# Filler products of x by ones on TensorE in the first adaLN of a decoder layer: with and without

## The chip, the cores and the metric

The kernel runs on one core of a Trainium2 chip. The metric is device time in microseconds (us) of one execution. It stands beside the span that the hardware profiler shows, which runs from the program's first instruction to its last. TensorE is called PE in the profile, VectorE DVE, ScalarE ACT, GpSimd POOL and SyncE, which issues most transfers here, SP.

## What is computed

One layer of a decoder trunk, for a prompt of 512 tokens and 8 single-token samples that share the weights, so 520 columns of activations with 1024 rows. All is fp32 in and out. Cut to what matters here:

```
m  = silu(c) @ ada_w + ada_b                     # 1024 x 6144; one c for the prompt, 8 for the samples
shift1, scale1, gate1, shift2, scale2, gate2 = split(m, 6)
h  = RMSNorm(x) * (1 + scale1) + shift1
z  = h @ w_in                                    # q, k, v, recurrent branch, gates
A  = RG-LRU branch(z) @ w_proj_a
B  = forgetting attention(z, paged cache) @ w_proj_b
x  = x + gate1 * ((sigmoid(gA) * A + sigmoid(gB) * B) @ w_o)
x  = x + gate2 * SwiGLU(RMSNorm(x) * (1 + scale2) + shift2)
y  = RMSNorm(x)
```

The change stands in the first line and the second: in how shift1 and scale1 are made, ahead of the first h.

## The kernel before, in words

Activations lie transposed: 8 tiles of 128 rows by 520 columns, taken in two halves of 260 columns (HALF) for each product. A large product is made of three fp32r products (high part by high part, low weights by high activations, high weights by low activations); ACT makes the high parts of the weights, DVE the low parts. PSUM is a pool of 8 banks, one product of 260 columns in each, taken in turn. The instructions' order on each engine follows the program's text, with a few places set by hand through `issue_after`.

The program opens as follows. SP issues, in this order: the parameters and constants, the 8 tiles of x (L100), 8 loads `araw` of 512 KB each of the first adaLN's weights (L479, `first_mod(0, ...)`, one for each block kq of 128 rows of c), three loads `wraw` of the first q weights (L525), and the 8 `araw` of the second half (`first_mod(1, ...)`). The tiles `araw` share 7 buffers with the cache pages.

Meanwhile PE sums the squares of x over the partitions by a product with ones (L559, `ss`), and then makes shift1 and scale1 for the first four row blocks: `first_mod(0, ...)` makes, for each kq, four products `adaf` of a 32-column silu(c) by 256 columns of `araw`, side by side in the four column groups of the array (L482; an fp32 product stands as two instructions in the profile, so a block kq is "x8"). `first_mod_end(0, ...)` copies the sum (ACT, `adas`, L495), transposes it (PE, `adaft`, L498), adds the bias (DVE, `mod`, L504) and makes the amplitude (DVE, `n1amp`, L508). `first_h` then makes h tile by tile: its high part `hh` on ACT (L514 for the prompt's columns, L518 for the samples', which come by way of POOL, L515 and L516) and its low part `hl` on DVE (L517, L519). `q_weights` splits the q weights (`whi` on ACT, L532; `wlo` on DVE, L533). Then come the first products of q over four row blocks (`qp`, L542), in groups of six banks; the 8 blocks of the second half of adaLN (`adaf` again) stand between them.

Inside this stretch stands `keep_busy` (L488 to L491). It makes n further fp32 products on PE, `idle`, of a 128x128 matrix of ones by the first 260 columns of x, each behind the one before, into a bank of its own that nothing reads. `first_mod(0, ...)` calls it with n = 1 behind each block kq from 2 to 7 (L485 and L486), and `first_mod_end(0, ...)` with n = 3 behind the transposes (L499 and L500).

Of the kernel before, what the change touches and what calls it, by code (L numbers as in the profile page):

```python
# [28 lines left out]
HALF = NT // 2  # L29
# [36 lines left out]
def kernel(ctx, tc, xT, par, gates, b_f, cst, cse, own, cache_k, cache_v, cache_lf, pt,  # L66
# [3 lines left out]
    pe, act, dve, pool, sp = nc.tensor, nc.scalar, nc.vector, nc.gpsimd, nc.sync  # L70
# [9 lines left out]
    def slot(name, cols=NT, dt=F32, parts=128):  # L80
        return heap.tile([parts, cols], dt, name=name, tag="slot")

    def bank(name, parts=128, cols=512):
        return psp.tile([parts, cols], F32, name=name, tag="bank")
# [9 lines left out]
    x = []  # L94
# [9 lines left out]
    ident = cs[:, C_ID:C_ID + 128]  # L104
    ones = cs[:, C_ONE:C_ONE + 128]
# [5 lines left out]
    silc = keep.tile([128, KT, 32], F32, name="silc")  # L111
# [47 lines left out]
    for jt in range(FF // 128):  # L159
# [5 lines left out]
        for name in BLOCKS:  # L165
            units.append((c, name, 4))
            if name in JOIN[jt]:
                g, i = JOIN[jt][name]
# [307 lines left out]
    def first_mod(fh, acc, kqs):  # L476
        for kq in kqs:
            raw = pgp.tile([128, 2, 512], F32, name="araw", tag="pg")
            sp.dma_start(raw, ada_w[kq * 128:kq * 128 + 128, :2048].rearrange("p (v c) -> p v c", v=2)  # L479
                         [:, :, 512 * fh:512 * fh + 512])  # L480
            for g in range(4):
                m = pe.matmul(acc[32 * g:32 * g + 32, :256], lhsT=silc[:, kq],  # L482
                              rhs=raw[:, g // 2, 256 * (g % 2):256 * (g % 2) + 256],
                              start=kq == 0, stop=kq == KT - 1, tile_position=(0, 32 * g))
            if fh == 0:  # L485
                keep_busy(m, 1 if kq > 1 else 0)  # L486

    def keep_busy(m, n):  # L488
        for _ in range(n):
            with tc.issue_after(m.ins):  # L490
                m = pe.matmul(idle[:, :HALF], lhsT=ones, rhs=x[0][:, :HALF], start=True, stop=True)  # L491

    def first_mod_end(fh, acc):
        sb = slot("adas", 256)
        act.copy(sb, acc[:, :256])  # L495
        tp = bank(f"adaft{fh}")
        for b in range(2):
            m = pe.transpose(tp[:, b * 128:b * 128 + 128], sb[:, b * 128:b * 128 + 128], ident)  # L498
        if fh == 0:  # L499
            keep_busy(m, 3)  # L500
        tv = tp[:, :256].rearrange("p (b g c) -> p b g c", b=2, g=4)
        fs = slice(4 * fh, 4 * fh + 4)
        for v in (1, 0):
            dve.tensor_tensor(  # L504
                mod[:, v, fs].rearrange("p (q b) c -> p b q c", b=2), tv[:, :, 2 * v:2 * v + 2, 0:9],
                prm[:, fs, P_AB + v:P_AB + v + 1].rearrange("p (q b) c -> p b q c", b=2).to_broadcast([128, 2, 2, 9]),
                ALU.add)
        dve.scalar_tensor_tensor(amp1[:, fs], mod[:, 1, fs], 1.0, prm[:, fs, P_N1:P_N1 + 1].to_broadcast([128, 4, 9]),  # L508
                                 ALU.add, ALU.mult)
# [35 lines left out]
    def wraw():  # L545
        return wp.tile([128, KT, 256], F32, name="wraw", tag="wraw", bufs=2)

    idle = bank("idle")
    ssq = [bank(f"ss1_{j}") for j in range(2)]
    for f in range(KT):  # L550
        t = slot("sq1")
# [5 lines left out]
        if f % 4 == 3:  # L557
            for j, (t0, t1) in enumerate(HALVES):
                pe.matmul(ssq[j][:, :HALF], lhsT=ones, rhs=sq[:, t0:t1], start=f == 3, stop=f == KT - 1)  # L559
    acc = [bank(f"adaf{fh}") for fh in range(2)]  # L560
    first_mod(0, acc[0], range(KT))
    r1 = slot("r1")
    for j, (t0, t1) in enumerate(HALVES):
# [6 lines left out]
    raw = wraw()  # L570
    q_weights(0, raw, 0, 0)
    first_mod_end(0, acc[0])
    for f in range(4):
        first_h(f)
# [3 lines left out]
    for g3 in (0, 3):  # L578
        banks = [bank(f"qp{i}_{j}") for i in range(g3, g3 + 3) for j in range(2)]
        for k in range(4):  # L580
            for n in range(6):
                q_matmuls(0, g3 + n // 2, n % 2, k, banks[n])
                if g3 == 0 and n == 5:
                    first_mod(1, acc[1], (2 * k, 2 * k + 1))
            if g3 and k == 0:
                first_mod_end(1, acc[1])
                for f in range(4, KT):
                    first_h(f)
        for n in range(6):
            t0, t1 = HALVES[n % 2]  # L590
            act.copy(qpart[g3 + n // 2][:, t0:t1], banks[n][:, :HALF])
        if g3 == 0:
            flr = slot("flr", KT * H).rearrange("p (k c) -> p k c", k=KT)
            sp.dma_start(flr, w_in[:, COL_FL:COL_FL + H].rearrange("(k p) c -> p k c", p=128))
# [325 lines left out]
    for i in range(KT):  # L920
        if i % 4 == 0:
            qtp.append(bank(f"qt{i}", NS))
        if i < 6:
            t = qpart[i]
            for j, (t0, t1) in enumerate(HALVES):
                b = bank(f"q{i}_{j}")
# [52 lines left out]
    g = [None] * KT  # L979
# [397 lines left out]
    g = None  # L1377
# [323 lines left out]
    for j in range(2):  # L1701
        for m in range(2 * PLAIN):
            if j == 0:
                begin(u + 3)
            b = bank(f"fi{m}_{j}")
# [88 lines left out]
```

## Time and profile before

| | us |
|---|---|
| three runs | 1015.08, 1015.64, 1018.36 |
| median | 1015.64 |
| the profiled execution, its own time | 1018.03 |
| its span | 1016.4 |
| PE busy in the span | 994.3 |
| DVE busy | 797.3 |
| ACT busy | 547.5 |
| mean granted clock of TensorE | 0.996 |

Rows of the timeline have the start in us, the duration, the engine, the source line, the operation, the tile written and those read, the shape and the number of instructions merged; behind it in brackets the engine's idle time before it and what ended it. Rows of the chain of work have the start, the length and the work; the chain leads back from the last instruction to whatever released each one. "SPq" is SP's queue issuing a transfer; "to landing" is the time from there until the data are in place. A row of windows has a stretch's ends and its length, PE's busy time with its instructions, the granted clock of TensorE as a share of the full one, the busy share of the DMA engines and GB/s.

### The profile page before, as it was taken

What the parts mean: (1) busy time and instruction counts of PE and PEld (TensorE: products, weight loads), DVE (VectorE), ACT (ScalarE), POOL (GpSimd) and SP (SyncE); (2) the same over time, 40 slices, a digit from 0 to 9 for tenths busy, and PEclk for the clock granted to TensorE, in tenths of its full rate; (3) what the DMA queues carried; (4) which work ended last, traced back from release to release, by engine and by line L of the source; (5) the groups of instructions that cost most, each with busy time, mean ns of one, the idle gap of its engine ahead of it and who ended that gap; (6) DMA issues with size and microseconds to landing.
All of it is one profiled execution on the core that took longest, in us unless ns stands there. A gap on an engine that the chain in (4) does not pass through costs nothing.

```text
span 1016.4 us, 21281 instructions
## 1 busy us (share of the span) xinstructions
PE 994.3 (98%) x8012; PEld 921.1 (91%) x8012; DVE 797.3 (78%) x1423; ACT 547.5 (54%) x1128; POOL 327.6 (32%) x415
## 2 busy tenths in 40 slices
PE   5999999999999999999999999999999999999996
PEld 2799999999998988888888888999999999999996
DVE  5559999998999888886655544869988888888764
ACT  4534576848761576777783233554444444445553
POOL 0346111121143245653400001583442442425112
PEclk9999999999999999999999999999999999999998
DMA  9798857788879998995867995324234243233122
GB/s 325 250 324 279 242 189 202 243 261 278 281 250 345 331 312 286 321 294 190 251 216 269 319 340 186 84 74 115 81 108 125 63 125 98 70 104 105 63 64 85
DMA packets 164378, 206.97 MB, mean 204 GB/s; under 512 B 9827, under 2 KB 125043, under 8 KB 164211
## 3 DMA queue, kind: packets, MB, share of 16 engines
q1 hardware_dynamic: 147634, 152.78, 48.1%
q0 software_dynamic: 12960, 46.41, 13.8%
q10 hardware_dynamic: 3680, 6.42, 1.7%
q8 instruction: 63, 1.03, 0.4%
q14 instruction: 41, 0.33, 0.1%
HBM read 192.49 MB, written 13.09 MB: 202 GB/s over the span
## 4 chain that ended last, share of the span: by engine, by line
PE 93%; DMA 2%; DVE 2%; ACT 1%; issue 0%; SPq 0%; POOL 0%; DVEq 0%; POOLq 0%; ACTq 0%
PE fo L307 12%; PE k L307 5%; PE wo L307 5%; PE gb L307 5%; PE gr L307 5%; PE v L307 5%; PE ga L307 5%; PE xr L307 5%; PE pb L307 4%; PE pv L839 3%; PE pa L307 3%; PE po L1302 2%; PE qp L542 2%; PE q L542 2%; PE ada L374 2%; PE ptt L1268 2%
## 5 line engine op out<-in xcount | busy, mean ns | idle before, releaser
L246 ACT CAST whi<-wraw 128x1024 fp32r<-128x1024 f32 (+1 forms) x79 | 82.0, 1039 | 113.6 <-PE pb L307 34.3
L248 DVE TENSOR_TENSOR wlo<-wraw,whi 128x1024 fp32r<-128x1024 f32 (+1 forms) x79 | 99.1, 1256 | 19.0 <-ACT whi L246 16.6
L307 PE MATMUL fo<-ach,wb 128*128 128x260 f32 x512 | 93.4, 283 | 0.0
L270 ACT CAST wb<-ws 128x512 fp32r<-128x512 f32 x72 | 44.7, 621 | 86.0 <-PE fo L307 58.9
L700 POOL DMA_DIRECT2D pg<-in_cache_k_dram x74 | 39.6, 536 | 143.1 <-DVE S L751 62.6
L271 DVE TENSOR_TENSOR wb<-wraw,wb 128x512 fp32r<-128x512 f32 x86 | 76.4, 889 | 4.7 <-ACT wb L270 3.9
L307 PEld LDWEIGHTS fo<-ach,wb 128*128 128x128 f32 x512 | 78.9, 188 | 0.0
L271 DVE TENSOR_TENSOR wb<-ws,wb 128x512 fp32r<-128x512 f32 x72 | 68.7, 954 | 12.6 <-ACT wb L270 11.0
L261 POOL TENSOR_TENSOR ws<-wraw 128x512 f32<-128x512 f32 x18 | 24.4, 1353 | 153.2 <-DMA wraw<-in_w_fi_dram 104.1
L307 PE MATMUL fo<-acl,wb 128*128 128x260 f32 x256 | 72.2, 282 | 0.0
L270 ACT CAST wb<-wraw 128x512 fp32r<-128x512 f32 x86 | 53.5, 622 | 31.4 <-ACT cp L1683 6.2
L750 DVE TENSOR_TENSOR pg<-pg,qb 128x1024 f32<-128x1024 f32 x48 | 57.9, 1221 | 2.5 <-DMA pg<-in_cache_k_dram 2.5
L751 DVE TENSOR_REDUCE S<-pg 128x16 f32<-128x1024 f32 x48 | 57.4, 1209 | 0.2
L1259 POOL TENSOR_SCALAR p<-p,mu 128x128 f32<-128x128 f32 (+3 forms) x28 | 38.4, 1381 | 53.0 <-DVE mu L1255 47.1
L307 PEld LDWEIGHTS fo<-acl,wb 128*128 128x128 f32 x256 | 48.2, 188 | 0.0
L1253 ACT ACTIVATE p<-p,mu 128x128 f32<-128x128 f32 (+3 forms) x64 | 35.4, 554 | 18.2 <-DVE mu L1252 18.0
L307 PE MATMUL v<-hh,whi 128*128 128x260 f32 x128 | 38.2, 298 | 0.8 <-ACT row L819 0.5
L307 PE MATMUL k<-hh,whi 128*128 128x260 f32 x128 | 37.3, 292 | 0.0
L307 PE MATMUL pb<-oh,whi 128*128 128x260 f32 x128 | 37.1, 290 | 0.2 <-ACT oh L1360 0.2
L307 PE MATMUL gb<-hh,whi 128*128 128x260 f32 x128 | 37.0, 289 | 0.0
L307 PE MATMUL v<-hl,whi 128*128 128x260 f32 x128 | 36.9, 288 | 0.0
L307 PE MATMUL v<-hh,wlo 128*128 128x260 f32 x128 | 36.9, 288 | 0.0
(1101 smaller groups left out, 3957.3 us busy)
## 6 DMA issues: line engine op xcount, KB each, us to landing
araw<-in_ada_w_dram SPq DMA_DIRECT2D x48, 512.0 KB, 7.6
wraw<-in_w_fi_dram SPq DMA_DIRECT2D x44, 512.0 KB, 5.3
pg<-in_cache_k_dram POOLq DMA_DIRECT2D x42, 512.0 KB, 6.2
pg<-in_cache_v_dram SPq DMA_DIRECT2D x42, 512.0 KB, 5.5
wraw<-in_w_in_dram SPq DMA_DIRECT2D x34, 512.0 KB, 6.4
wraw<-in_w_in_dram SPq DMA_DIRECT2D x11, 1024.0 KB, 8.5
pg<-in_cache_v_dram POOLq DMA_DIRECT2D x22, 512.0 KB, 6.1
pg<-in_cache_k_dram POOLq DMA_DIRECT2D x32, 256.0 KB, 5.9
```

The lines of the kernel that those rows point to most:

```text
L246: state["act"] = act.copy(hi[:, :k1 - k0], src)
L248: state["last"] = dve.tensor_tensor(lo[:, :k1 - k0], src, hi[:, :k1 - k0].bitcast(F32), ALU.subtract)
L270: state["act"] = act.copy(t[:, :4], src)
L271: state["last"] = dve.tensor_tensor(t[:, 4:], src, t[:, :4].bitcast(F32), ALU.subtract)
L307: state["mm"] = pe.matmul(out[:, :t1 - t0], lhsT=wt[k], rhs=at, start=k == 0 and m == 0, stop=k == nk - 1 and m == 2)
L542: state["mm"] = pe.matmul(b[:, :HALF], lhsT=wt, rhs=at[:, t0:t1], start=k == 0 and m == 0, stop=k == 3 and m == 2)
L700: done.append(eng.dma_start(pg, cache[bass.ds(r, 1), :, c0:c1].rearrange("a p c -> (a p) c")))
L750: dve.tensor_tensor(pg, pg, q, ALU.mult)
L751: last = dve.tensor_reduce(S[r // 2][:, c:c + H], pg.rearrange("p (h d) -> p h d", d=DH), AX.X, ALU.add)
L839: pe.matmul(pv[0][32 * gq:32 * gq + 32, :], lhsT=pw[r][:, c:c + 32], rhs=pgs[gq // 2][:, 512 * hf:512 * hf + 512], start=j == 0, stop=j == ...
L1253: act.activation(p[:, :n + 128], p[:, :n + 128], AF.Exp, bias=mu[:, 0:1], scale=-1.0, accum_out=mu[:, 1:2])
L1259: (pool.tensor_scalar(p, p, mu[:, 2:3], None, ALU.mult) if a and i + 1 < KT else act.activation(p, p, AF.Copy, scale=mu[:, 2:3]))
```

## The change

The nine filler products, the function that makes them and their bank go. The other instructions keep their order on every engine; line numbers behind the function fall by 10 (L559 becomes L549, L542 becomes L533).

```
-                m = pe.matmul(acc[32 * g:32 * g + 32, :256], lhsT=silc[:, kq],
+                pe.matmul(acc[32 * g:32 * g + 32, :256], lhsT=silc[:, kq],
                               rhs=raw[:, g // 2, 256 * (g % 2):256 * (g % 2) + 256],
                               start=kq == 0, stop=kq == KT - 1, tile_position=(0, 32 * g))
-            if fh == 0:
-                keep_busy(m, 1 if kq > 1 else 0)
-
-    def keep_busy(m, n):
-        for _ in range(n):
-            with tc.issue_after(m.ins):
-                m = pe.matmul(idle[:, :HALF], lhsT=ones, rhs=x[0][:, :HALF], start=True, stop=True)
...
         for b in range(2):
-            m = pe.transpose(tp[:, b * 128:b * 128 + 128], sb[:, b * 128:b * 128 + 128], ident)
-        if fh == 0:
-            keep_busy(m, 3)
+            pe.transpose(tp[:, b * 128:b * 128 + 128], sb[:, b * 128:b * 128 + 128], ident)
...
-    idle = bank("idle")
     ssq = [bank(f"ss1_{j}") for j in range(2)]
```

On PE, in the first adaLN, rows stand as follows before, from block kq = 2 to the start of kq = 4 (what a row waits for is in brackets; DMAHW are the semaphores by which a load tells that it has landed):

```order
L482 MATMUL adaf_143<-araw,silc 32x256 [waits DMAHW6_49]
L482 MATMUL adaf_143<-araw,silc 32x256 x3
L491 MATMUL idle<-x,cs 128x260 [waits DMAHW2_49]
L482 MATMUL adaf_143<-araw,silc 32x256 [waits DMAHW7_49]
L482 MATMUL adaf_143<-araw,silc 32x256 x3
L491 MATMUL idle<-x,cs 128x260
L482 MATMUL adaf_143<-araw,silc 32x256 [waits DMAHW0_49]
```

and in the changed kernel, at the same place:

```order
L482 MATMUL adaf_142<-araw,silc 32x256 [waits DMAHW6_49]
L482 MATMUL adaf_142<-araw,silc 32x256 x3
L482 MATMUL adaf_142<-araw,silc 32x256 [waits DMAHW7_49]
L482 MATMUL adaf_142<-araw,silc 32x256 x3
L482 MATMUL adaf_142<-araw,silc 32x256 [waits DMAHW0_49]
```

Each block now stands directly behind the one before, and its first row waits for its own load as it did.

On PE, from the last filler between blocks to the first products of q, before:

```order
L491 MATMUL idle<-x,cs 128x260
L498 MATMUL adaft_230<-cs,adas 128x128 [waits Activation_49]
L498 MATMUL adaft_230<-cs,adas 128x128
L491 MATMUL idle<-x,cs 128x260 x3
L542 MATMUL qp_0_286<-hh,whi 128x260 [waits Activation_49]
L542 MATMUL qp_0_286<-hh,wlo 128x260 [waits DVE_49]
```

and in the changed kernel:

```order
L482 MATMUL adaf_142<-araw,silc 32x256 x3
L491 MATMUL adaft_223<-cs,adas 128x128 [waits Activation_49]
L491 MATMUL adaft_223<-cs,adas 128x128
L533 MATMUL qp_0_276<-hh,whi 128x260 [waits Activation_49]
L533 MATMUL qp_0_276<-hh,wlo 128x260 [waits DVE_49]
```

The transposes stand directly behind the last block of adaLN, and the first product of q directly behind the transposes; the waits of these rows are the same. DVE, ACT, POOL and SP have the same rows with the same waits in both kernels.

## The prediction

> **What bounds the kernel now.** I read the page first: the busy shares, the row of the granted clock, and the chain that ended last.
>
> ```profile
> PE 994.3 (98%) x8012; PEld 921.1 (91%) x8012; DVE 797.3 (78%) x1423; ACT 547.5 (54%) x1128; POOL 327.6 (32%) x415
> PEclk9999999999999999999999999999999999999998
> PE 93%; DMA 2%; DVE 2%; ACT 1%; issue 0%; SPq 0%; POOL 0%; DVEq 0%; POOLq 0%; ACTq 0%
> ```
>
> PE is busy for 98% of the span and makes 93% of the chain. What delays PE's first products of q by 1 us therefore delays the end by about 1 us, and the change has to be judged by when PE comes to those products and how fast it then goes. Busy time alone does not tell whether the work was needed, so I went on to the chain in the first 45 us.
>
> ```profile
> 12.93 2.10 PE ss L559 x4
> 15.03 2.72 PE adaf L482 x24
> 17.75 0.65 PE idle L491 x2
> 18.40 0.57 PE adaf L482 x8
> 18.97 0.64 PE idle L491 x2
> ...
> 23.22 0.57 PE adaf L482 x8
> 23.79 0.64 PE idle L491 x2
> 24.42 0.31 PE adaft L498 x2
> ...
> 26.48 0.21 ACT hh L518
> 26.69 0.04 issue
> 26.73 3.39 PE qp L542 x24
> 30.12 0.57 PE adaf L482 x8
> 30.69 0.91 PE qp L542 x6
> 31.60 0.57 PE adaf L482 x8
> ...
> 44.15 6.46 PE qp L542 x54
> ```
>
> Two things are to be seen. The fillers stand in the chain: six of them, 0.64 us each, 3.9 us in all. And the clock changes under them: up to 17.75 a block of adaLN takes 2.72 / 3 = 0.91 us, afterwards 0.57. So TensorE started at a low clock and came to its full one at about 17.7. The page's row of the clock does not show it, since it reads 9 from the first slice on; the durations do.
>
> **The first part of the change: PE no longer spends 3.9 us on fillers.** What is late next is the loads. These are rows of SP's queue, each an issue and its time to landing, for the blocks kq = 1 and kq = 7 of the first half, the second load of q weights, and kq = 1 of the second half.
>
> ```profile
> L479 SPq DMA_DIRECT2D araw<-in_ada_w_dram x1: 374/374/374, 8.5 to 8.5; - x1
> DMA to landing us min/median/max: 5.3/5.3/5.3
> ...
> L479 SPq DMA_DIRECT2D araw<-in_ada_w_dram x1: 368/368/368, 16.1 to 16.1; - x1
> DMA to landing us min/median/max: 5.9/5.9/5.9
> ...
> L525 SPq DMA_DIRECT2D wraw<-in_w_in_dram x1: 512/512/512, 17.0 to 17.0; - x1
> DMA to landing us min/median/max: 8.0/8.0/8.0
> ...
> L479 SPq DMA_DIRECT2D araw<-in_ada_w_dram x1: 1179/1179/1179, 20.2 to 20.2; - x1
> DMA to landing us min/median/max: 10.2/10.2/10.2
> ```
>
> Block 1 lands at 8.5 + 5.3 = 13.8 and block 7 at 16.1 + 5.9 = 22.0, so a block lands each 8.2 / 6 = 1.37 us, and the blocks 3 to 6 at about 16.5, 17.9, 19.3 and 20.6. Before, block 7 was multiplied at 23.22, 1.2 us after it had landed. So of the 3.9 us only 1.2 can come back there; the rest turns into waits of PE for loads. Earlier consumption frees the buffers of `araw` earlier and SP could issue sooner, but that moves no landing: the DMA engines are full in this stretch (share 1.04, 382 GB/s, in the row 17.74 to 21.15 further down). I cost that edit at nothing, and the filler's bank too: it takes away a wait of one q product for PE itself.
>
> From block 7 on, the path to q's products goes over other engines. This is the timeline of that stretch.
>
> ```profile
> 23.85 0.37 ACT L495 COPY adas<-adaf 128x256 f32<-128x256 f32 x1 [8.31 <-PE adaf L482]
> 24.12 1.14 ACT L532 CAST whi<-wraw 128x512 fp32r<-128x512 f32 x2
> 24.75 0.30 DVE L504 TENSOR_TENSOR mod<-adaft,prm 128x36 f32<-128x36 f32 x2 [1.62 <-PE adaft L498]
> 25.22 0.81 ACT L514 ACTIVATE hh<-xn,mod,n1amp 128x512 fp32r<-128x512 f32 x1
> 25.26 0.58 POOL L515 TENSOR_TENSOR hr<-xn,n1amp 128x8 f32<-128x8 f32 x1 [24.02 <-DVE n1amp L508]
> 26.08 0.39 PE L542 MATMUL qp<-hh,whi 128*128 128x260 f32 x1
> ```
>
> With a full clock, block 7 would run from 22.0 to 22.6, the copy to 23.05, the transposes to 23.4, and the path over DVE and POOL, 26.73 - 24.73 = 2.0 us long, would end at 25.4. ACT is later: its copy is followed by the casts of the first q weights, whose load has no landing in the trace. It was issued between block 7 (landed 22.0) and the second load of q weights (17.0 + 8.0 = 25.0), so by even spacing it lands at about 23.5; the cast at 24.12 bounds it from above. Casts of 1.14 us to 24.65, `hh` of 0.81 us to 25.45, its second piece of 0.21 to 25.7. So PE comes to the 24 products of the chain at about 25.7, not 26.73: **1.0 us earlier**, between 0.45 (load at 24.12) and 1.2 (all of block 7's slack). The next block of the second half, wanted at 31.60 before and landed at 20.2 + 10.2 = 30.4, leaves 1.2 us, enough for it. The three fillers behind the transposes lay in time in which PE waited for ACT and POOL; in themselves they are worth nothing.
>
> **The second part: what the gaps do to the clock.** Here the trace has another place to read, later in the kernel. I asked for windows of 3.41 us, the length of the one stretch at half clock:
>
> ```profile
> 10.91:14.32 3.41, 2.74 (x7) 1.00 1.02 371
> 14.32:17.74 3.41, 3.41 (x27) 1.00 1.05 398
> 17.74:21.15 3.41, 3.41 (x32) 1.00 1.04 382
> ...
> 458.06:461.47 3.41, 2.80 (x15) 1.00 0.94 293
> 461.47:464.88 3.41, 3.41 (x16) 0.50 1.01 332
> ```
>
> At 461.47 the clock fell to 0.50 for exactly one window. In the window before it PE was busy for 2.80 of 3.41 us, and its longest waits were short ones, by the timeline:
>
> ```profile
> 459.39 0.39 PE L1245 MATMUL sc<-ksA,qqA 128*128 128x256 f32 x1 [0.16 <-DVE pl L1273]
> 461.38 0.53 PE L307 MATMUL v<-hh,whi 128*128 128x260 f32 x1 [0.26 <-DVE pl L1273]
> ```
>
> So 82% of busy time, in small products, was too little to keep the full clock, and one window that was full brought it back. At the start it is the same: the window up to 14.32, 80% busy, was followed by half speed, the full one up to 17.74 by full speed. In the changed kernel PE works for 0.57 us of each 1.37 from about 18.9 to 22.0 (42%), and from 22.6 to 25.5 for the 0.31 us of the transposes. Every window that lies in there is far below 82%. I therefore take it that **the clock is at half when q's products begin**, and that it comes back at the end of the first window that lies wholly in them.
>
> The price: block 7 takes 0.91 instead of 0.57 us and the transposes some 0.15 more, so the path over POOL ends at 25.9, and PE starts 0.85 us earlier than before, not 1.0. A product then takes 3.41 / 16 = 0.213 us, against 6.46 / 54 = 0.120. The first window that begins behind 25.5 ends between 28.9 and 32.3, as the window's edges happen to fall; the middle is 30.6. By then (30.6 - 25.9) / 0.213 = 22 of the 24 products are made, the other two take 0.24, and the block behind them is reached at 30.8 instead of 30.12: **0.7 us later**. With the window's end at 28.9, 14 are made at half speed and ten take 1.2 us, so 30.1: no change. At 32.3 the 24 products end at 31.0, the block at 31.9, two of the six products behind it run at half speed and four do not, 32.8 instead of 31.60: 1.2 us later. The sum is +0.7 us, between 0 and +1.2.
>
> A rule speaks against this step. The Trainium skill (TensorE: Matmul & The Clock Gate, "HAM oscillation — how this bites in real kernels") puts the danger at gaps in which PE idles for more than about 3.4 us. The longest gap of the changed kernel would be some 2 us, so by that rule the clock would stay full and only the gain would be left; the row at 461.47, where the clock fell behind waits of 0.16 and 0.26 us, disagrees with it.
>
> **The rivals.** B: the clock stays full through the gaps. Then the first part alone counts, -1.0 us, 1014.6. For it: after 17.74 the changed kernel's PE is never idle for longer than about 2 us, and the fall at 461.47 is a single case. Against it: that single case had far more work in its window than this stretch will have. C, the slower side: the clock does not come back after one window, because q's first products wait for `hh`, `whi` and `hl` in between, as they did before at full clock (24 products in 3.39 us, where 24 x 0.120 is 2.9). A window 80% busy was not enough at 10.91. Each further window costs 3.41 x (1 - 0.120 / 0.213) = 1.5 us: +2.2 with one more, 1017.8, +3.7 with two, 1019.3. It passes a loss of 3 us when the full clock comes later than about 36 us. Against it: at half clock PE is the slower party, so the waits should vanish, and both openings in this trace came after one full window.
>
> **How the numbers follow.** The sum is made against the profiled execution, 1018.03 us with 1.6 of it outside its span of 1016.4; with +0.7 that execution would take 1018.7. It stands 2.4 above the median of the runs. The difference is carried to the median: 1015.64 + 0.7 = 1016.3. I give the forecast 0.58, B 0.20 and C 0.22. The runs of before lie from 0.6 below to 2.7 above their median; where the windows of the clock fall in an execution is one thing that could make that, since a window at half clock costs 1.5 us, and it blurs each case. The range, 1014.0 to 1019.2, takes in B with the lower spread, and C up to two windows. About 0.3%, 3.05 us, is what a measurement of this kernel can tell from no change. Of the forecast I put 0.51 within it, 0.05 above and 0.02 below; of B 0.15 within and 0.05 below; of C 0.09 within and 0.13 above. Together: faster 0.07, same 0.75, slower 0.18.
>
> **What would show it.** In the changed kernel's trace PE's rows of `adaf` should start 1.37 us apart with idle time before them that a load ends, the last at 22.0; the first long run of `qp` should start at 25.7 to 25.9; windows from about 20 to 31 should show a granted clock of 0.50, and the 24 products should take near 4.9 us instead of 3.39. Products of 0.120 us from 25.7 on would speak for B; half speed beyond 36 us for C. I am wrong in the first step if block 7 does not land at 22, and in the whole if PE has time to give back later, so that a start 1 us later does not reach the end: a wait for a transfer that PE does not set off itself would do that.

## The result, and the profile after

The changed kernel took 1020.66 us in the median of five runs (1019.05 to 1021.2), the kernel before 1016.19 beside it (1015.08 to 1018.36). The ratio of the runs is 1.0034, with a 95% interval of 1.0020 to 1.0048. That is some 3.4 us slower. The time lies 1.5 us above the end of the stated range, 1019.2; about 0.55 of that is the kernel before, which came out at 1016.19 and not at the 1015.64 that the range was reckoned from. Four more comparisons of the same kernel, further down, gave 1.0017, 1.0035, 1.0015 and 1.0019; weighted by the inverse squares of their intervals the five give 1.0024, give or take 0.0006, or **2.5 us**.

The page of the changed kernel, the same three rows as before:

```profile
PE 992.5 (97%) x7994; PEld 919.7 (90%) x7994; DVE 797.9 (78%) x1423; ACT 547.8 (54%) x1128; POOL 327.0 (32%) x415
PEclk8899999999999999999999999999999999999998
PE 90%; DVE 5%; ACT 2%; DMA 1%; issue 1%; SPq 0%; POOL 0%; DVEq 0%; ACTq 0%
```

The clock's row now begins with two eights: the full clock is missing for a part of the first 50 us. Its chain through the same stretch (start, length, work):

```profile
16.16 7.81 DMA araw<-in_ada_w_dram
23.98 0.04 issue
24.02 1.12 PE adaf L482 x8
25.14 0.02 issue
25.16 0.38 ACT adas L488
25.55 0.04 issue
25.59 0.70 PE adaft L491 x2
...
26.78 0.82 ACT hh L505
27.60 0.04 issue
27.64 6.15 PE qp L533 x26
33.79 0.57 PE adaf L482 x8
```

Where the fillers stood, the chain leads through a load. The first products of q start at 27.64, and the block behind them, which started at 30.12 before, at 33.79. PE's timeline tells how it came to that:

```profile
17.24 0.64 PE L482 MATMUL adaf<-araw,silc 128*32 128x256 f32 x8 [0.43 <-DMA araw<-in_ada_w_dram]
18.60 0.64 PE L482 MATMUL adaf<-araw,silc 128*32 128x256 f32 x8 [0.72 <-DMA araw<-in_ada_w_dram]
19.93 1.08 PE L482 MATMUL adaf<-araw,silc 128*32 128x256 f32 x8 [0.70 <-DMA araw<-in_ada_w_dram]
...
24.02 1.08 PE L482 MATMUL adaf<-araw,silc 128*32 128x256 f32 x8 [0.29 <-DMA araw<-in_ada_w_dram]
```

The blocks come every 1.36 us, each behind a wait for its load, and from 19.93 on a block takes 1.08 instead of 0.64. The windows show the clock beside PE's busy time:

```profile
16.51:19.92 3.41, 1.58 (x24) 1.00 1.04 395
19.92:23.34 3.42, 2.85 (x24) 0.50 1.07 367
23.34:26.75 3.41, 2.15 (x14) 0.50 1.09 362
26.75:30.16 3.41, 2.52 (x10) 0.50 1.05 385
30.16:33.58 3.42, 3.42 (x18) 0.50 1.05 387
33.58:36.99 3.41, 3.41 (x33) 1.00 0.85 276
```

Behind a window with 1.58 us of work the clock fell, stayed at half for four windows, and came back behind the first that was full, at 33.58. Six of those 13.7 us fall on products of q.

One thing in this execution has, as the runs below show, nothing to do with the fillers. This is SP's issue of block 7:

```profile
L479 SPq DMA_DIRECT2D araw<-in_ada_w_dram x1: 368/368/368, 16.2 to 16.2; - x1
DMA to landing us min/median/max: 7.8/7.8/7.8
```

It landed at 24.0, where it had landed at 22.0 in the profile of before.

### The profile page after: what moved, and what is told of

It reads as the page before. It is cut to its first block, busy times and chain, and to the rows that moved or that the text cites. A ratio compares the mean times of both kernels' runs of the same rounds, so it can differ in the third digit from the quotient of the medians.

```text
span 1019.0 us, 21245 instructions
## 1 busy us (share of the span) xinstructions
PE 992.5 (97%) x7994; PEld 919.7 (90%) x7994; DVE 797.9 (78%) x1423; ACT 547.8 (54%) x1128; POOL 327.0 (32%) x415
## 4 chain that ended last, share of the span: by engine, by line
PE 90%; DVE 5%; ACT 2%; DMA 1%; issue 1%; SPq 0%; POOL 0%; DVEq 0%; ACTq 0%
PE fo L307 12%; PE wo L307 5%; PE gb L307 5%; PE xr L307 5%; PE pb L307 4%; PE ga L307 4%; PE k L307 4%; PE v L307 4%; PE gr L307 3%; PE pa L307 3%; PE pv L829 3%; PE qp L533 2%; PE po L1292 2%; PE q L533 2%; PE ada L374 2%; PE ptt L1258 2%
## 5 line engine op out<-in xcount | busy, mean ns | idle before, releaser
L271 DVE TENSOR_TENSOR wb<-wraw,wb 128x512 fp32r<-128x512 f32 x86 | 74.2, 863 | 5.5 <-ACT wb L270 4.7
L271 DVE TENSOR_TENSOR wb<-ws,wb 128x512 fp32r<-128x512 f32 x72 | 64.6, 897 | 13.6 <-ACT wb L270 11.9
L307 PE MATMUL pa<-gh,wlo 128*128 128x260 f32 x128 | 36.2, 284 | 0.7 <-DVE wlo L248 0.7
L307 PE MATMUL xr<-hh,whi 128*128 128x260 f32 x128 | 36.7, 287 | 0.0
```

The lines of the kernel that those rows point to most:

```text
L271: state["last"] = dve.tensor_tensor(t[:, 4:], src, t[:, :4].bitcast(F32), ALU.subtract)
L307: state["mm"] = pe.matmul(out[:, :t1 - t0], lhsT=wt[k], rhs=at, start=k == 0 and m == 0, stop=k == nk - 1 and m == 2)
```

## The experiments

Two theories stood at first. The **clock theory** is the prediction's: the gaps close the clock, and the loss is q's first products at half speed. The **load theory** holds that the loads land 2 us later in the changed kernel and PE, with nothing to hide it, waits. All ratios below are against the kernel before on the same chip, with 95% intervals; 0.0010 is 1.0 us. "Mean clock" is the mean over the runs of a comparison; it was 0.997 for the kernel before in each of them.

**Only the six fillers between blocks.**

```
-        if fh == 0:
-            keep_busy(m, 3)
```

> The kernel before with the six fillers between the blocks kept and the three behind the transposes left out. Clock theory (the loss of the changed kernel is work done at half clock, because the gaps close the clock): one gap of about 1.4 us, from the transposes at 24.7 to the first product of q at 26.1, leaves the window that holds it some 60% busy, so the clock falls for one window in most executions; a window of q products at half clock costs up to 1.5 us: 0.5 to 1.5 us over the kernel before. Load theory (the changed kernel is slower because its adaLN loads land about 2 us later, 24.0 instead of 22.0, and PE waits for them): the fillers do nothing for the loads, block 7 lands at 24 in this kernel only by chance, and the time is that of the kernel before within 0.5 us.

1.0012 (1.0003 to 1.0022), mean clock 0.9957. The three fillers behind the transposes, which lie beside waits of PE and by the prediction's reckoning cost and bring nothing in themselves, are worth about 1.2 us. That speaks for the clock; in the one execution traced it stayed full all the same.

**Only the three fillers behind the transposes.**

```
-            if fh == 0:
-                keep_busy(m, 1 if kq > 1 else 0)
```

> The three fillers behind the transposes kept, the six between the blocks left out. Clock theory: the clock is at half when the three fillers run, they take 2.6 us instead of 1.3 and push the first product of q back by up to 1.2 us, while the window that brings the clock back fills 1.3 us earlier; the sum is no better than the changed kernel, 3 to 5 us over the kernel before, with half clock shown from about 20 to 31. Load theory: as the changed kernel, with block 7 landing near 24.

0.9998 (0.9986 to 1.0010), mean clock 0.9955: a miss of the clock theory's numbers. The windows of the one execution traced show how it can be (window, length, PE busy, clock):

```profile
17.34:20.75 3.41, 1.87 (x28) 1.00 1.05 389
20.75:24.16 3.41, 2.02 (x21) 1.00 1.08 354
24.16:27.57 3.41, 2.91 (x19) 1.00 1.07 371
```

1.87 and 2.02 us of 3.41 did not lose the clock here, and the gap behind block 7 is filled by the three fillers. But in the changed kernel's first trace a window of the same blocks with 1.58 us lost it before block 7 began, and in its third, below, one with 1.74 did. So the blocks alone lie at the edge, one side or the other by how the windows fall on them, and a mean clock of 0.9955 says that other executions of this kernel did lose it.

**Fillers from block 4 on, and three behind the transposes.**

```
-                keep_busy(m, 1 if kq > 1 else 0)
+                keep_busy(m, 1 if kq > 3 else 0)
```

> The kernel before without the fillers behind the blocks 2 and 3, so with four between blocks and three behind the transposes. Clock theory: PE has the blocks 3 and 4 back to back and is then kept 88% busy, every window stays full, the clock stays; block 7 starts when it lands instead of up to 1.2 us later: 0 to 1.0 us under the kernel before, by how early its loads land. Load theory: a share of the changed kernel's loss, 0.5 to 1.5 us over the kernel before.

0.9986 (0.9975 to 0.9997), mean clock 0.9969: faster than the kernel before by 1.4 us. In its chain the load of the first q weights is what comes last, as the prediction had it for a full clock:

```profile
16.39 7.01 DMA wraw<-in_w_in_dram
23.41 0.02 issue
23.43 1.14 ACT whi L532 x2
24.57 0.73 ACT hh L514
25.30 0.04 issue
25.34 3.77 PE qp L542 x26
29.11 0.57 PE adaf L482 x8
```

26 products in 3.77 us, against 6.15 in the changed kernel.

**The changed kernel again**, without an edit.

> The changed kernel once more, for a second trace of where its loads land and where its clock falls. Clock theory: 3 to 4.5 us over the kernel before; landing of block 7 anywhere between 22 and 24, by chance; half clock from about 20 or 23 to the end of the first window filled by q products. Load theory: block 7 lands at 24 again while the other kernels of this call show 22.

1.0017 (1.0007 to 1.0026), mean clock 0.9927. Block 7 landed at 21.8 here, so the load theory falls: 24.0 was chance. Over all traces it landed between 21.8 and 24.0, and at 24.0 in a kernel with fillers too (those behind the blocks 6 and 7 only). In this trace the clock fell only when q had begun:

```profile
22.48:25.90 3.42, 1.10 (x9) 1.00 1.09 356
25.90:29.31 3.41, 3.41 (x18) 0.50 1.05 386
```

1.10 us of work, in the window that holds the gap behind block 7, lost it for one window. Ahead of it two windows of blocks, with 2.06 and 1.91 us, had kept it. The first block behind q's products started at 30.15, no later than in the profile of before.

**All nine fillers, of 8 columns.**

```
-                m = pe.matmul(idle[:, :HALF], lhsT=ones, rhs=x[0][:, :HALF], start=True, stop=True)
+                m = pe.matmul(idle[:, :8], lhsT=ones, rhs=x[0][:, :8], start=True, stop=True)
```

> The kernel before with all nine fillers in their places, but each of 8 columns instead of 260. Clock theory: their work is far too little to hold the clock, so the gaps close it as in the changed kernel, and the time is that of the changed kernel, 1.5 to 3 us over the kernel before, with a mean clock near 0.993 instead of 0.997. Order theory (the fillers help by where they stand, as something that holds PE back and lets q's products start packed): the time is that of the kernel before within 0.7 us.

1.0006 (0.9994 to 1.0018), mean clock 0.9941, between both, and a miss of the clock theory's 1.5 to 3 us. The time alone would fit the order theory; the trace does not:

```profile
23.01:26.42 3.41, 1.98 (x16) 1.00 1.08 363
26.42:29.84 3.42, 3.42 (x19) 0.50 1.05 384
```

The clock fell as in the last case, behind 1.98 us of busy time, more than the 1.87 that had kept it above, and the block behind q's products started at 30.53, 0.5 us later than before. A product of 8 columns stands as 0.39 us in the timeline, so busy time seems to overstate what short products do for the clock.

**Later loads, in the changed kernel and in the kernel before.**

```
+    for n in range(2):
+        sp.dma_start(slot("late", 512), ada_w[128 * n:128 * n + 128, 5632:6144])
     first_mod(0, acc[0], range(KT))
```

> The changed kernel with two more loads of 256 KB each, of weights that nothing reads, between the loads of the blocks 1 and 2 of adaLN, so that all later loads land 1.4 us later. Load-bound theory (PE has no work in hand in this stage and the delay reaches the end): 1.4 us over the changed kernel, 3.3 to 4.5 over the kernel before. Give-back theory (a later limit, the page sums and weight splits of DVE from 80 to 100 us, hides what PE loses or gains here): within 0.5 us of the changed kernel.

> The same two loads in the kernel before. Its PE had 1.2 us of slack at block 7 and its ACT 0.6 at the first q weights. Load-bound theory: 0.2 us from block 7, but the first casts of q weights start at 24.9 instead of 24.1, so 0.5 to 1.0 us over the kernel before. Give-back theory: within 0.4 us of the kernel before.

In the changed kernel 1.0038 (1.0025 to 1.0051), 1.4 us above its pooled 1.0024, give or take 1.4; in the kernel before 1.0010 (1.0001 to 1.0020). Both are the numbers of the load-bound theory: a later load reaches the end, whole without fillers, less its slack with them. The intervals are too wide to rule out that some of it is given back. If it holds, chance in the loads is part of the spread of every comparison here.

**Twelve fillers behind the transposes.**

```
-            keep_busy(m, 3)
+            keep_busy(m, 12)
```

> The kernel before with twelve fillers behind the transposes instead of three: 9 x 0.437 = 3.9 us more of PE, at full clock, which end at 29.8; q's 24 products then run packed and end at 32.7 instead of 30.1, 2.5 us later, with no half clock. If a delay of PE here reaches the end: 2.0 to 2.8 us over the kernel before. Give-back theory: 0.5 to 1.5 us.

1.0039 (1.0026 to 1.0052). In the trace the block behind q's products started 2.6 us later than in the profile of before, at a full clock. Nothing of it is given back by the end; the comparison, 4.0 us, shows more than the trace's lag, and the expected 2.0 to 2.8. A slower stretch behind 546 us, found further down, makes 0.7 of the difference.

**The changed kernel a third time, and the kernel before against itself.**

> The changed kernel a third time, for a third trace of when block 7 lands, when q's products start and how long they run at half clock. If the half clock is the loss: mean clock 0.992 to 0.994, time 1.5 to 2.5 us over the kernel before; in the trace, the place of the first adaLN block behind q's first products equals its start plus 0.2 us for each product at half clock. If the first comparison (3.4 us) was right in size: 3 us or more.

> The kernel before against itself, to see what such a comparison gives for no change, and for a second trace of it: a ratio of 0.9990 to 1.0010, a mean clock of 0.997, block 7 landing anywhere from 21.8 to 24.0, and no half clock between 18 and 60 us.

The first gave 1.0035 (1.0023 to 1.0047), mean clock 0.9930, as large a loss as the first comparison; the second 1.0009 (0.9997 to 1.0021), which is what no change looks like here. In the third trace of the changed kernel the load was punctual and the clock's return as forecast, so it is the one to size the price by. Its chain, and its windows:

```profile
22.38 1.13 PE adaf L482 x8
...
26.01 5.99 PE qp L533 x26
32.00 0.57 PE adaf L482 x8
```

```profile
17.94:21.35 3.41, 1.74 (x28) 1.00 1.05 381
21.35:24.77 3.42, 2.24 (x18) 0.50 1.09 349
24.77:28.18 3.41, 2.17 (x9) 0.50 1.06 379
28.18:31.60 3.42, 3.42 (x18) 0.50 1.06 390
31.60:35.01 3.41, 3.41 (x33) 1.00 1.03 382
```

**Fillers behind the blocks 6 and 7 only; fillers of half the width.**

```
-                keep_busy(m, 1 if kq > 1 else 0)
+                keep_busy(m, 1 if kq > 5 else 0)
```

```
-                keep_busy(m, 1 if kq > 1 else 0)
+                keep_busy(m, 1 if kq > 3 else 0, 130)
```

> Fillers behind the blocks 6 and 7 only, and the three behind the transposes. Clock theory: the stretch from 20.6 on is kept full, the blocks 3 to 5 leave gaps of some 0.7 us in which the clock may fall in some executions but comes back before q begins; PE comes to block 7 when it lands. 0.5 to 1.5 us under the kernel before, as the kernel with four fillers between blocks. If the clock is lost for long by the gaps of blocks 3 to 5: the time of the kernel before or 0.5 over.

> Four fillers between blocks, behind the blocks 4 to 7, but of 130 columns, and three of 260 behind the transposes. If half the filler's work holds the clock: 1.0 to 2.0 us under the kernel before, no worse than with fillers of 260 columns. If not: closed windows before q in part of the executions, mean clock 0.995 or 0.996, 0 to 0.7 us under the kernel before.

0.9989 (0.9977 to 1.0000) and 0.9993 (0.9984 to 1.0002), mean clocks 0.9970 and 0.9977. By trace and mean clock two fillers hold the clock as well as four, and half the width too; with them PE starts block 7 when it lands, and the gain that the prediction saw behind a full clock, 1.0 us, is what these kernels show, 0.7 to 1.4 us, though by intervals that reach to no change for the last two.

**Two more traces each of the changed kernel and of the one with fillers from block 4 on**, to see where the rest of the loss is made.

> The changed kernel, a fourth trace. If the whole loss is made in q's first products: the first block of the second adaLN half starts 2.5 to 3.5 us later than in the kernel with four fillers between blocks, and from there to the end both take the same within 1 us. If a part is lost later: 1 to 2 us at the start and 1 us or more behind 100 us, again in waits for DVE or for pages.

> The kernel with fillers behind the blocks 4 to 7 and three behind the transposes, again: PE waits for the same loads as in the changed kernel, at a full clock. Half-clock theory: its 26 first products of q take 3.7 to 3.8 us against 4.9 to 6.2 in the changed kernel, no half clock between 18 and 60 us.

> The changed kernel, a fifth trace. As the fourth: the loss in q's first products by itself, or a further 1 us behind 100 us.

> The kernel with fillers behind the blocks 4 to 7 and three behind the transposes, a third trace; block 7 landing between 21.8 and 24.0, q's 26 first products in 3.7 to 3.8 us, the rest of the span as in the changed kernel within 1 us if the loss is made at the start alone.

Ratios: 1.0015 (0.9995 to 1.0035) and 1.0019 (1.0001 to 1.0036) for the changed kernel, mean clock 0.9922 and 0.9923; 0.9993 (0.9971 to 1.0016) and 0.9981 (0.9963 to 1.0000) for the other, 0.9965 and 0.9971. All traces of three kernels, in us; "block" is the first block of the second adaLN half, "rest" the span's remainder behind its start, and "half clock" that within q's products. Starts are the timeline's; the block's is 0.07 earlier there than in the chain:

| kernel | block 7 starts | q starts | block starts | half clock | rest |
|---|---|---|---|---|---|
| changed | 24.02 | 27.64 | 33.72 | 5.9 | 985.3 |
| changed | 21.85 | 25.24 | 30.08 | 3.4 | 987.8 |
| changed | 22.38 | 26.01 | 31.93 | 5.6 | 987.6 |
| changed | 22.19 | 25.71 | 30.67 | 3.5 | 987.6 |
| changed | 22.14 | 25.52 | 31.38 | 5.7 | 988.5 |
| before | 23.15 | 26.08 | 30.05 | 0 | 986.3 |
| before | 22.95 | 25.89 | 29.86 | 0 | 984.5 |
| from block 4 on | 21.96 | 25.34 | 29.04 | 0 | 984.3 |
| from block 4 on | 23.57 | 26.95 | 30.62 | 0 | 986.5 |
| from block 4 on | 22.11 | 25.47 | 29.16 | 0 | 984.9 |

On the mean the block starts at 31.56 in the changed kernel and at 29.96 before: **1.6 us later**, where the forecast had 0.7. In the four traces whose block 7 landed by 22.3 it starts at 31.02, 1.1 later. Against the kernel with fillers from block 4 on, which waits for the same loads at a full clock, the 31.56 are 1.95 later. The rest is longer too, by 2.0 us against the mean of before and by 2.1 against the other, though in the first trace it is not.

A part of that belongs to the changed program and not to chance. These are PE's windows between the same two DVE instructions, the first `mixl` and the last `r3p`, before and in the changed kernel's first trace:

```profile
545.75:1008.02 462.27, 461.49 (x3803) 1.00 0.42 130
547.75:1010.65 462.90, 462.11 (x3803) 1.00 0.42 130
```

The same PE instructions take 0.6 us longer, at a full clock and with PE busy throughout. The length is 462.85 to 462.90 in all five traces of the changed kernel, and 462.21 to 462.33 in twelve of the thirteen others, among them the changed kernel with later loads; only the kernel with twelve fillers has 462.96. So it is neither half clock nor the missing fillers as such. What in the program makes it is not shown.

What else the rest holds scatters. A window of half clock near 463 us, 1.5 us, stands in three of the five traces, in one of the two of before and in one of the other three. The third trace loses 2.2 us behind 290 us, in waits for DVE and for a page. The second, fourth and fifth lose 0.9 to 1.6 us at 79 to 104 us. There PE waits for DVE, here in the fifth:

```profile
90.07 0.39 PE L307 MATMUL xr<-hh,wlo 128*128 128x260 f32 x1 [1.28 <-DVE wlo L248]
```

and DVE had waited for a load of queries, there to 79.19 and in the profile of before to 75.98 (1.3 of the 3.2 us between them are the later start of the block):

```profile
79.19 2.47 DVE L736 TENSOR_TENSOR pg<-pg,qb 128x1024 f32<-128x1024 f32 x2 [2.60 <-DMA qb<-qtd]
```

```profile
75.98 2.36 DVE L746 TENSOR_TENSOR pg<-pg,qb 128x1024 f32<-128x1024 f32 x2 [3.31 <-DMA qb<-qtd]
```

The same waits stand in traces of kernels with fillers, and whether the change makes them longer is not shown.

## Why the prediction was wrong

- **Loads are what is late next: right.** In all five traces block 7 starts 0.04 to 0.05 us behind its landing. That a full clock would leave a gain of 1.0 us was right as well: with fillers from block 4 on the block starts at 29.04 and 29.16 where block 7 landed by 22.1, 0.8 to 0.9 before the mean of before, and the five comparisons of kernels that wait for the loads with the clock held gained 0.7 to 1.9, though four of their intervals reach to no change.
- **Block 7 at 22.0: right in the middle, but no fixed number.** It landed at 21.8 to 22.3 in four traces of the changed kernel and at 24.0 in the fifth. The prediction took one execution's landing as the kernel's and gave its chance no width; in the changed kernel nothing hides such a delay from q's start. The one late landing of five makes 0.5 of the 1.6 us.
- **The clock is at half when q's products run: right**, in every trace of the changed kernel, for 3.4 to 5.9 us of them, and it came back behind the first full window. In the second trace it fell 0.7 us after q had begun, and in that and the fifth only the window with the gap behind block 7 lost it, not those of the blocks. C, a longer loss, did not happen: 33.58 was late because q started late. B is out: in the third trace the clock fell at 21.35 behind a window whose gaps were 0.72 us at most. The trace does not agree with the rule that the danger begins with idle gaps of more than about 3.4 us (the Trainium skill, TensorE: Matmul & The Clock Gate, "HAM oscillation — how this bites in real kernels").
- **The reading of the threshold: wrong in size.** The 82% at 458 us were not a bound; of the windows that hold blocks of adaLN alone, those with 53 to 60% of busy time (1.82 to 2.06 us, five of them in all traces) kept the clock, and those with 46 to 51% (1.58 to 1.74 us, four) lost it. That the clock falls did not hang on it, since the gap behind block 7 lies below either; when it falls did.
- **The price of half clock: the term of the sum that was mis-sized.** "By then 22 of the 24 products are made": the 24 were those of one row of the chain of before, which begins at 26.73, while PE had made two more from 26.08 on. From its own start PE has 26 to make. And the prediction let them run without waits at half clock. In the third trace q started at 26.01, as forecast, and the clock came back at 31.60, inside the forecast's bounds. By its reckoning the 24 end at 31.0; measured, the block started at 31.93. Of these 0.9 us two products are 0.43, the later start is 0.1, and the remaining 0.4 are waits between the first products. Put into the forecast's own sum, with the clock back at its middle, 30.6: (30.6 - 26.0 - 0.4) / 0.213 = 20 products at half clock, six more in 0.7 us, the block at 31.3, so **1.2 us later instead of 0.7**, against 1.1 in the four traces with a punctual load.
- **Two terms stood at nothing, and together they weigh more.** One is the landing's chance, 0.5 us on the mean of these traces. The other is all that lies behind the block: the sum ends there, and takes what follows as unchanged without a row for it. From 546 us on the changed kernel loses 0.6 us in every trace.
- **What stays open:** the comparisons show 2.5 us, give or take 0.6; the traces 1.6 at the start and 0.6 behind 546 us, so 2.2. Why that stretch is slower is not known. Between the block and 546 us the traces scatter by some 2 us with any kernel, and these runs do not tell a loss from chance there.

## What to carry to other kernels

Work without a result can pay when it fills a gap just ahead of a dense stretch: what counts is the clock in which the dense stretch begins, and here three fillers in the one long gap kept it in the execution traced, and with two more just ahead the mean clock was that of the kernel before (0.9970), while the fillers further ahead stood in the way of PE. Price a lost clock from where the engine really begins, with every product still to be made, and not from a row of the chain that begins later. Take a landing time from several executions, since one trace can be 2 us off. And do not end the sum at the place of the edit: a quarter of this loss lay 500 us behind it.

## What the runs showed of the hardware

Short products hold the clock badly for the busy time that they show: with fillers of 8 columns it fell behind 58% of busy time, where windows of adaLN blocks alone kept it with 53 to 60%. The landing of the same load, block 7's, issued within 0.6 us, differed by 2.2 us between executions. And a kernel compared with itself came out at 1.0009 (0.9997 to 1.0021), so a single comparison here tells little below 0.2%. The same 3803 PE instructions, at a granted clock of 1.00, took 462.2 to 462.3 us in nine programs and 462.9 to 463.0 in two, the same in every trace of one program to within 0.05 us.
